# One plan for the attention part and the feed-forward part, and two-operand products of VectorE written as a ScalarE scaling and a sum

## The chip, the cores and the metric

The kernel runs on one core of one Trainium2 chip. The metric is the device time of the kernel in microseconds (us), the median of three runs. TensorE (PE) does the matmuls and the transposes against an identity; VectorE (DVE), ScalarE (ACT) and GpSimd (POOL) do the elementwise work; SyncE (SP) issues nearly all DMAs. An engine runs its instructions in the order in which they stand in its queue, so what a queue holds first is waited for first.

## The reference

One layer of a residual trunk on 2048 rows of width 1024, in float32. Cut to what matters:

```python
u = rms_norm(h, norm1_w)
dq, dk, dv, sq, sk, sv = split(u @ w_in)
# 4 differential heads: two softmax maps per head, T5 position bias, chunk-causal mask
p = softmax(q[c] @ k[c].T * scale + bias)           # c = 0, 1
y_diff = rms_norm((p[0] - lam * p[1]) @ dv)
# 8 stick-breaking heads: strictly causal, no softmax
rem = reverse_cumsum(log_sigmoid(-z)) - log_sigmoid(-z)
y_sb = rms_norm(exp(log_sigmoid(z) + rem) @ sv)
h = h + concat(y_diff, y_sb) @ w_out
u2 = rms_norm(h, norm2_w)
h = h + (silu(u2 @ w_gate) * (u2 @ w_up)) @ w_down   # 1024 -> 2816 -> 1024
```

## The kernel before

**Arithmetic.** A float32 product is made of float16 matmuls: each operand is split into a high half (`hi`, a cast) and a low half (`lo`, operand minus `hi`), and three products are summed in PSUM. Weights are scaled by a power of two first: `split_weight` writes `hi = st * sW` on ACT, DVE or POOL, and `lo = st * sW - hi` with one DVE instruction, SCALAR_TENSOR_TENSOR, which scales its first operand by a per-row value and combines it with a second tensor.

**Attention part.** There are eight groups of heads: groups 0 to 3 are the differential heads (the "diff stage" below), groups 4 to 7 pairs of stick-breaking heads. Rows come in 16 tiles of 128. For each group `load_w` fetches the columns of `w_in` into `wst` and splits them into `w`; `proj_tile` or `proj_turned` projects (`pj` in PSUM), `proj_out` and `proj_batch` normalise and split q and k (`raw` holds four tiles of q and k; `rs` is their reciprocal norm). `diff_attn.probs(i)` handles row tile i: scores `sc` in PSUM, evacuated by DVE into `z` with a running maximum (`mx`), an exponential on ACT with its sum, and then `z0 = z0 + z1 * rc`, which joins the two maps; `split_t` casts the result into `s` (hi), subtracts (lo), and a transposing DMA makes `aT`, which `pv` multiplies with `v` into `yp`. Values of tile i are taken up when two later tiles have been scored. `out_proj` multiplies with `w_out` (`wo`, PSUM `po`, sum in `xf`), and `post` makes from tiles 0 to 11 what the feed-forward part reads (`xcd`).

**Feed-forward part.** Two halves of 8 row tiles, 11 steps of 256 hidden columns each; each 2x2 block product is done with seven products (`quad` for gate and up, `down`). In the first half `load_ffn` fetches each weight into one of two `stages`, squares it on ACT into `sq` (one buffer, used again for sums of the blocks), lets PE sum the columns (`fsc`), finds the scale on DVE, makes the block sums on POOL and splits into `wg`, `wu`, `wd`; it stores the result (`split`), and the second half reads it back. `build_x` does for tiles 12 to 15 what `post` does for the others.

**What sets the order.** In the attention part nothing is issued as it is written. `Recorder` notes every instruction with its reads and writes; `order` then lays them out by a list schedule with prices from `price`, a key (place in the program less a bonus), free buffers, and one more rule: an instruction that `price` marks with `port` (POOL's wide ones, and DVE's wide ones without PSUM operands) starts only when no other such one runs. Where code calls `either` (in `to16`, `tt`, `split_weight`, `split_psum`), the plan picks the engine, by when it would be done there with its price times `KW`. `issue` then emits the instructions in that order. The feed-forward part and tiles 12 to 15 of `out_proj` are outside of the plan: their order comes from the framework's own scheduler, and engines there are chosen by `pick`, which evens out running sums.

Of the kernel before, what the change touches and what calls it, by code (L numbers as in the profile page):

```python
# [40 lines left out]
KW = {"A": 1.0, "D": 2.5, "P": 0.6}  # L41
# [23 lines left out]
class Bank:  # L65


    def __init__(self, rec, pool, shape, dtype, kw):
# [10 lines left out]
        self.readers, self.ops, self.last, self.keep = [], {}, None, False  # L79
# [153 lines left out]
class Recorder:  # L233


    def __init__(self, tc):
        self.tc, self.on, self.ops, self.boost, self.behind, self.open, self.probe = tc, False, [], 0, [], None, None

# [30 lines left out]
    def price(self, eng, name, args, kw):  # L269
# [19 lines left out]
        if eng == "D":  # L289
# [6 lines left out]
            if n <= 16:  # L296
                return 200, None, None, False
# [5 lines left out]
        return (min(190 + 1.91 * n, 430 + 1.45 * n) if name == "tensor_tensor" else 165 + 0.9 * n), None, None, True  # L303
# [90 lines left out]
    def start(self):  # L394
        self.on, self.ops, self.banks = True, [], {}

    def order(self):
        ops = self.ops
        for o in ops:
            o.deps.discard(o.n)  # L400
            o.users, o.left, o.first, o.last, o.after = [], len(o.deps), [], [], 0.0
        for o in ops:
            for d in o.deps:
                ops[d].users.append(o)
        queue, room, held = {}, {}, {}
        for b in sorted(self.banks, key=lambda b: next(iter(b.ops))):
            b.first = ops[next(iter(b.ops))]
            b.first.first.append(b)
            queue.setdefault(b.slot, []).append(b)
            room[b.slot] = b.cap  # L410
            held[b] = len(b.ops)
            for o in b.ops:
                ops[o].last.append(b)
        events = [(0.0, n, "ready", o) for n, o in enumerate(ops) if not o.left]
        heapq.heapify(events)
        count = len(ops)
        ready = {e: [] for e in "TADPS"}
        till = dict.fromkeys(ready, 0.0)
        ring, table, done, shared, want = 0.0, None, [], 0.0, None
# [83 lines left out]
        assert len(done) == len(ops), (len(done), len(ops), [(e, [(o.n, o.calls[0][0].__name__) for o in r[:3]]) for e, r in ready.items()])  # L503
        self.span = now
        return done

    def issue(self):

        done = self.order()
        self.on = False  # L510
        with self.tc.manual_schedule():
            for o in done:
                for f, args, kw in o.calls:
                    o.out = f(*map(true, args), **{k: true(v) for k, v in kw.items()})  # L514


def block(tc, a, out):
# [4 lines left out]
    with top:  # L522
# [59 lines left out]
        make_identity(nc, id32[:])  # L582
        rec.start()
# [82 lines left out]
        def split_weight(hi, lo, st, n, sW, engines="P"):  # L666
# [46 lines left out]
        with ExitStack() as ph1:  # L713
# [38 lines left out]
            def load_w(g, st=None):  # L752
# [12 lines left out]
                for k in range(0, KT, kn):  # L765
                    ks = slice(k, k + kn)
                    split_weight(wv[:, 0, ks, :], wv[:, 1, ks, :], st[:, ks, :], 384 * kn, sW, "ADP" if first else "P")
# [122 lines left out]
            def proj_batch(g, G, B):  # L890
                st, v, raw = B
                qT, kT = new_qk()
                if g < 4:
# [9 lines left out]
                    DVE.tensor_tensor(rq, rq, rsb, ALU.mult)  # L903
# [127 lines left out]
            def diff_attn(g, G):  # L1031
                @pri("at")
                def probs(i):
# [43 lines left out]
                    for (b, n, z0), (_, _, z1) in zip(*zs):  # L1077
                        DVE.scalar_tensor_tensor(z0[:, :n], z1[:, :n], rc[:], z0[:, :n], op0=ALU.mult, op1=ALU.add)
# [255 lines left out]
            def load_wo(n):  # L1334
# [15 lines left out]
                for q, st in enumerate(sts):  # L1350
                    o = slice(D * q, D * q + D)
                    split_weight(hi[:, o], lo[:, o], st[:, :D], D, sW, "AP")
# [8 lines left out]
            def out_proj():  # L1361
                for t in range(NT):
# [20 lines left out]
                    SP.dma_start(hd[t], xf)  # L1383
                    if t >= 12:
                        yield
                        continue
                    post(t, xf)
                    yield

            held = []  # L1390
# [25 lines left out]
            while outs < 12:  # L1416
# [4 lines left out]
        with ExitStack() as ph2:  # L1421
            ps2 = ph2.enter_context(tc.tile_pool(name="ps2", bufs=2, space=PSUM, reuse_waits="tile"))
            fw = ph2.enter_context(tc.tile_pool(name="fw", bufs=2, reuse_waits="tile"))
            xops = {}

            def open_x(os):
                for o in os:
                    xops[o] = ph2.enter_context(tc.tile_pool(name=f"xp{o}", bufs=1, reuse_waits="tile"))
# [464 lines left out]
```

## Time and profile before

| | |
|---|---|
| median of 3 runs | 2657.18 us (2653.93 to 2659.12) |
| the profiled execution's own time | 2652.51 us |
| its span, first to last instruction | 2650.7 us |
| mean granted TensorE clock | 0.988 |
| PE busy | 2475.5 us (93%) |
| DVE busy | 1834.4 us (69%) |
| POOL busy | 1412.5 us (53%) |
| ACT busy | 1224.7 us (46%) |

PE's busy time is nearly the span, so the time that can be had lies in PE's idle 175 us and in stretches at a lower clock. The other engines' shares are means over stages that differ much; they have to be read stage by stage. In the rows of the profile L514 is the line that emits the plan and L220 the line through which all else passes, so instructions are told apart by their tiles.

### The profile page before, as it was taken

Reading aid. Unit: us, or ns where it says so; the run is one execution under the profiler, and the core shown is the slowest. Engines: PE = TensorE matmul, PEld = TensorE weight load, DVE = VectorE, ACT = ScalarE, POOL = GpSimd, SP = SyncE. Lnnn points to the kernel's source line nnn. Section 1 sums busy time; section 2 is a strip of 40 time slices with the busy share of each in tenths; the row PEclk is TensorE's granted clock in tenths of the full one; section 3 lists DMA queues with packets and bytes.
Section 4 is the critical chain, followed back from the end, with each engine's and each line's share of the span. In section 5 each row is a group of like instructions: output and inputs, shape, how many; then the busy total and the mean of one; then the engine's idle time right before and its main releaser. Section 6 shows DMA issues by size and latency. Waiting matters only on the chain.

```text
span 2650.7 us, 50621 instructions
## 1 busy us (share of the span) xinstructions
PE 2475.5 (93%) x19940; PEld 1510.4 (57%) x19940; DVE 1834.4 (69%) x3398; ACT 1224.7 (46%) x2365; POOL 1412.5 (53%) x1093
## 2 busy tenths in 40 slices
PE   6998999989899998899998899999999999999999
PEld 4555556568787875678773344444444444444444
DVE  7888888888888888775557767768685444444434
ACT  4566565656677767664434533435342112111121
POOL 3576675654454545366767757667574232332323
PEclk9999999999999999999998999999999999999999
DMA  7787797876898979888885665565649653545432
GB/s 242 188 181 157 160 191 162 184 155 139 181 189 181 189 175 194 209 189 222 223 321 210 219 225 221 212 230 203 251 170 360 255 210 138 212 152 193 183 112 96
DMA packets 557759, 522.35 MB, mean 197 GB/s; under 512 B 414208, under 2 KB 486400, under 8 KB 547280
## 3 DMA queue, kind: packets, MB, share of 16 engines
q1 hardware_dynamic: 555696, 517.03, 69.3%
q8 instruction: 156, 2.56, 0.4%
q0 software_dynamic: 512, 1.36, 0.1%
q10 hardware_dynamic: 1312, 0.72, 0.1%
q14 instruction: 83, 0.68, 0.1%
HBM read 261.08 MB, written 147.32 MB: 154 GB/s over the span
## 4 chain that ended last, share of the span: by engine, by line
PE 53%; DVE 11%; POOL 8%; DMA 7%; issue 6%; ACT 5%; SPq 0%; DVEq 0%; POOLq 0%; ACTq 0%
PE pd L220 18%; PE pj L514 9%; PE pm L220 8%; PE pa L220 5%; PE sc L514 5%; PE yp L514 4%; DMA aT<-s 3%; DVE z L514 3%; PE po L514 3%; POOL s L514 2%; DVE cg L220 2%; DVE wd L220 2%; ACT z L514 1%; DVE wu L220 1%; POOL sq L220 1%
## 5 line engine op out<-in xcount | busy, mean ns | idle before, releaser
L514 PE MATMUL pj<-w,xt 128*128 128x384 f16 (+1 forms) x3072 | 435.6, 288 | 10.5 <-DVE w L514 6.4
L220 PE MATMUL pd<-wd,act 128*128 128x512 f16 x1764 | 392.5, 380 | 11.1 <-ACT cg L220 4.3
L514 POOL TENSOR_TENSOR s<-z,s 128x512 f16<-128x512 f32 (+7 forms) x231 | 301.2, 1316 | 134.2 <-ACT s L514 113.0
L514 PE MATMUL sc<-kT,qT 128*128 128x512 f16 (+3 forms) x1280 | 320.7, 350 | 31.7 <-DVE z L514 22.4
L514 PEld LDWEIGHTS <-xt 128*128 128x128 f16 x3072 | 255.9, 99 | 142.7 <-issue 18.5
L220 POOL TENSOR_TENSOR act<-cg,act 128x512 f16<-128x512 f32 x126 | 172.8, 1382 | 272.9 <-ACT act L220 160.8
L220 PEld LDWEIGHTS <-wg 128*128 128x128 f16 x1848 | 182.2, 99 | 233.9 <-issue 16.7
L220 PEld LDWEIGHTS <-wu 128*128 128x128 f16 x1848 | 180.6, 98 | 216.2 <-DVE wu L220 2.5
L220 PEld LDWEIGHTS <-act 128*128 128x128 f16 x1764 | 172.8, 98 | 220.8 <-issue 15.2
L514 PE MATMUL yp<-v,aT 128*128 128x64 f16 (+1 forms) x4872 | 235.9, 204 | 28.6 <-DMA aT<-s 17.4
L514 PEld LDWEIGHTS <-aT 128*128 128x128 f16 x4896 | 218.6, 99 | 63.3 <-DMA aT<-s 25.8
L220 POOL TENSOR_TENSOR hs<-hs,cu 128x512 f32<-128x512 f32 x99 | 130.7, 1328 | 171.3 <-DVE hs L220 71.6
L514 POOL TENSOR_TENSOR z<-z,z 128x512 f16<-128x512 f32 (+4 forms) x108 | 117.5, 1090 | 150.3 <-ACT z L514 135.0
L220 ACT CAST act<-cg 128x512 f16<-128x512 f32 x126 | 77.3, 617 | 240.5 <-DVE cg L220 210.2
L220 PE MATMUL pm<-X,wu 128*128 128x512 f16 x792 | 179.9, 379 | 1.5 <-DVE wu L220 1.5
L220 PE MATMUL pm<-X,wg 128*128 128x512 f16 x792 | 180.2, 381 | 0.0
L220 DVE SCALAR_TENSOR_TENSOR hs<-pd,c,hs 128x512 f32<-128x512 f32 x136 | 98.3, 746 | 110.0 <-PE pd L220 81.0
L514 ACT ACTIVATE z<-z,ng 128x1024 f32<-128x1024 f32 (+4 forms) x192 | 170.9, 891 | 3.3 <-ACT ng L514 0.4
L514 DVE TENSOR_TENSOR_SCAN z<-z,sc 128x512 f32<-128x512 f32 x128 | 162.2, 1273 | 14.2 <-ACT z L514 10.7
L514 PEld LDWEIGHTS <-qT 128*128 128x128 f16 x1280 | 113.6, 98 | 99.2 <-issue 32.9
L514 DVE TENSOR_SCALAR_CACHE_REDUCE z<-sc,c 128x512 f32<-128x512 f32 (+3 forms) x256 | 159.9, 649 | 10.6 <-PE sc L514 9.2
L514 PE MATMUL pj<-xt,w 128*128 128x128 f16 x2304 | 152.8, 219 | 13.1 <-DVE qT L514 4.4
(262 smaller groups left out, 4687.3 us busy)
## 6 DMA issues: line engine op xcount, KB each, us to landing
xt<-xs SPq DMA_DIRECT2D x112, 512.0 KB, 4.1
hs<-hd SPq DMA_DIRECT2D x68, 512.0 KB, 4.5
hd<-hs SPq DMA_DIRECT2D x56, 512.0 KB, 4.1
split<-wg SPq DMA_DIRECT2D x11, 1792.0 KB, 8.1
split<-wu SPq DMA_DIRECT2D x11, 1792.0 KB, 6.8
split<-wd SPq DMA_DIRECT2D x11, 1792.0 KB, 7.6
wg<-split SPq DMA_DIRECT2D x11, 1792.0 KB, 7.4
wd<-split SPq DMA_DIRECT2D x11, 1792.0 KB, 11.8
```

The costliest lines, as they stand in the source:

```text
L220: return f(*map(true, args), **{k: true(v) for k, v in kw.items()})
L514: o.out = f(*map(true, args), **{k: true(v) for k, v in kw.items()})
```

## The change

**The plan spans the kernel.** `start` no longer throws away what was recorded. There are three plans one after the other, each starting from the state that the last one left: the attention part with all 16 tiles of `out_proj`; then the first two weights of the feed-forward part (`wg`, `wu` of step 0) and the first six blocks of `X`; then all the rest. Within each plan instructions move freely; on each engine all of one plan stand ahead of the next one's. `w_gate` and `w_up` of step 0 and the six blocks `X` are fetched from ACT's queue, not SP's.

**Products.** For odd row tiles i of the diff stage `z0 + z1 * rc` becomes a scaling of `z1` on ACT and a sum by DVE or POOL, as the plan picks. For groups 1 to 7 of `w_in` and for `w_out`, `split_weight` scales `st` in place on ACT, casts `hi`, and subtracts on DVE or POOL. The product `raw * rs` may go to DVE or POOL.

**Prices.** `KW` of DVE goes from 2.5 to 4 (so a choice shuns DVE more), small DVE instructions from 200 to 220 ns, and POOL's tensor_tensor loses the cheaper slope above some 520 elements.

```diff
-KW = {"A": 1.0, "D": 2.5, "P": 0.6}
+KW = {"A": 1.0, "D": 4, "P": 0.6}
...
-                return 200, None, None, False
+                return 220, None, None, False
...
-        return (min(190 + 1.91 * n, 430 + 1.45 * n) if name == "tensor_tensor" else 165 + 0.9 * n), None, None, True
+        return (190 + 1.91 * n if name == "tensor_tensor" else 165 + 0.9 * n), None, None, True
...
     def start(self):
-        self.on, self.ops, self.banks = True, [], {}
+        self.on, self.base, self.banks, self.open = True, len(self.ops), {}, None
...
-        def split_weight(hi, lo, st, n, sW, engines="P"):
+        def split_weight(hi, lo, st, n, sW, engines="P", spread=False):
+            if spread:
+                ACT.mul(st, st, sW[:])
+                to16(hi, st, n, engines)
+                tt(lo, st, hi, ALU.subtract, n)
+                return
...
-                    DVE.tensor_tensor(rq, rq, rsb, ALU.mult)
+                    tt(rq, rq, rsb, ALU.mult, 1024)
...
-                        DVE.scalar_tensor_tensor(z0[:, :n], z1[:, :n], rc[:], z0[:, :n], op0=ALU.mult, op1=ALU.add)
+                        if i % 2:
+                            ACT.mul(z1[:, :n], z1[:, :n], rc[:])
+                            tt(z0[:, :n], z0[:, :n], z1[:, :n], ALU.add, n)
+                        else:
+                            DVE.scalar_tensor_tensor(z0[:, :n], z1[:, :n], rc[:], z0[:, :n], op0=ALU.mult, op1=ALU.add)
...
-            while outs < 12:
+            while outs < NT:
                 next(op)
                 outs += 1
             rec.issue()
...
         with ExitStack() as ph2:
-            ps2 = ph2.enter_context(tc.tile_pool(name="ps2", bufs=2, space=PSUM, reuse_waits="tile"))
+            rec.start()
+            ps2 = Pool(rec, ph2.enter_context(tc.tile_pool(name="ps2", bufs=2, space=PSUM, reuse_waits="tile")), 2, True)
...
+                q = ACT if f0 == 0 and nme != "d" else SP
...
             load_now(0, 0, "g", W)
-            load_x(0, XL[:3])
-            next(op)
-            next(op)
+            load_x(0, XL[:3], ACT)
             load_now(0, 0, "u", W)
-            load_x(0, XL[3:6])
...
+            load_x(0, XL[3:6], ACT)
+            for dst, xf in late:
+                SP.dma_start(dst, xf)
...
+            rec.issue()
             pjs.close()
+            rec.start()
```

Counted over the built program, PE's instructions are the same in kind and number. Of the 48 products `z0 + z1 * rc` of odd tiles POOL gets 47 sums; POOL gets all 16 of `raw * rs`, all 14 low halves of `w`, and 6 low halves of `wo`; 18 casts into `s` go from POOL to ACT.

**Where it shows, 1: the third diff group, row tile 11.** DVE's queue before, with the two products of this tile (1024 and 512 columns wide) right behind `rc`, and the product `raw * rs` of a projection:

```order
L514 TENSOR_REDUCE sums_5278<-s_5628 128x2
L514 RECIPROCAL rc_5712<-sums_5278 128x1
L514 SCALAR_TENSOR_TENSOR v_5703<-pj_5630,v_5703 128x128
L514 TENSOR_SCALAR rc_5712<-rc_5712,c_347,sums_5278 128x1
L514 SCALAR_TENSOR_TENSOR z_5455<-z_5513,rc_5712,z_5455 128x1024
L514 SCALAR_TENSOR_TENSOR z_5480<-z_5599,rc_5712,z_5480 128x512
L514 TENSOR_TENSOR raw_5390<-raw_5390,rs_5699 128x1024
```

POOL's queue now, where the sums of the same tile stand (`z_5492` and `z_5524` are its two pieces), with a `raw * rs` ahead of the first and splits of q and k between them:

```order
L525 TENSOR_TENSOR rs_5665<-rs_5665,mh_100 128x16
L525 TENSOR_TENSOR raw_5224<-raw_5224,rs_5665 128x1024
L525 TENSOR_TENSOR z_5492<-z_5492,z_5540 128x1024
L525 TENSOR_TENSOR raw_5224<-raw_5224,gk 128x4x128
L525 TENSOR_SCALAR s_5854<-z_5492 128x1024
L525 TENSOR_TENSOR st_5593<-raw_5224,st_5593 128x4x2x64
L525 TENSOR_TENSOR s_5854<-z_5492,s_5854 128x1024
L525 TENSOR_TENSOR st_5593<-raw_5224,st_5593 128x4x2x64
L525 TENSOR_TENSOR z_5524<-z_5524,z_5580 128x512
```

Three wide DVE instructions are gone from behind `rc`; the two sums now stand apart from each other in POOL's queue, and the splits of their results behind them in the same queue.

**Where it shows, 2: the start of the feed-forward part, ACT.** Before, with `sq` the squares of the three weights of step 0 in turn and `x` the last casts of `post`:

```order
L220 ACTIVATE sq_21532<-stages 128x2048
L514 CAST x_21482<-z_21476 128x2x512
L220 ACTIVATE wg_21534<-stages,c_21531 128x2x512
L514 CAST x_21486<-z_21259 128x512
L220 ACTIVATE wg_21534<-sq_21532,c_21531 128x2x512
L220 ACTIVATE sq_21791<-stages 128x2048
```

And now, from the last cast of `post` on (`X` are the blocks that PE reads, `wu` the second weight):

```order
L525 CAST x_21709<-z_21301 128x512
L525 DMA stages<-in_w_gate_dram 128x8x256
...
L525 DMA X_22027<-xcd_73 128x4096
L525 ACTIVATE sq_22031<-stages 128x2048
L525 DMA stages<-in_w_up_dram 128x8x256
L525 ACTIVATE wg_22064<-stages,c_22060 128x2x512
L525 ACTIVATE wg_22064<-sx_22033,c_22060 128x512
L525 ACTIVATE sq_22074<-stages 128x2048
L525 ACTIVATE wu_22102<-stages,c_22099 128x2x512
```

The squares of `wg` and `wu` are still ACT's, but both stand behind all of `post`, and six fetches of `X` stand ahead of the first.

**The same place, PE.** PE's queue now, from the last matmul of `out_proj` (tile 15) to the first product of the feed-forward part (`fsc_22041` are the column sums of `wg`, `fsc_22080` those of `wu`):

```order
L525 MATMUL po_21932<-wo_18551,mt_21690 128x256
L525 LDWEIGHTS ones
L525 MATMUL fsc_22041<-sq_22031,ones 128x256
...
L525 MATMUL fsc_22080<-sq_22074,ones 128x256
L525 LDWEIGHTS wg_22064
L525 MATMUL pa_22129<-X_22017,wg_22064 128x512
```

Before, the column sums of `wg` stood in the middle of tile 13 of `out_proj`, and those of `wu` in that of tile 14, so that matmuls stood between them and the first product; now none does, and both column sums stand ahead of it.

More of the change, by code (lines that the diff above doesn't have):

```diff
@@ L502, in order @@
                 heapq.heappush(events, (end, count, "end", o))
-        assert len(done) == len(ops), (len(done), len(ops), [(e, [(o.n, o.calls[0][0].__name__) for o in r[:3]]) for e, r in ready.items()])
-        self.span = now
+        assert len(done) == len(new), (len(done), len(new), [(e, [(o.n, o.calls[0][0].__name__) for o in r[:3]]) for e, r in ready.items()])
+        self.ring, self.table, self.shared, self.span = ring, table, shared, now
         return done
@@ L510, in issue @@
         self.on = False
[L511 to L514, printed above, removed]
+        for o in done:
+            for f, args, kw in o.calls:
+                o.out = f(*map(true, args), **{k: true(v) for k, v in kw.items()})
 def block(tc, a, out):
@@ L582, in block @@
         make_identity(nc, id32[:])
+        top.enter_context(tc.manual_schedule())
         rec.start()
@@ L1455, in stage @@
                 f0 = 256 * fg
-                with tc.issue_after(rows[1].ins) if (fg, nme) == (1, "u") else nullcontext():
+                with rec.issue_after(rows[1].ins) if (fg, nme) == (1, "u") else nullcontext():
                     fetch(st, f0, nme)
```

81 lines of the change are left out of this document (47 added, 34 removed).

## The prediction

> **What bounds the kernel now.** I read the page's head and its line of busy times first, then busy time by stretches of the span, then PE's waits in each stretch, and last the groups of instructions for prices.
>
> ```profile
> span 2650.7 us, 50621 instructions
> PE 2475.5 (93%) x19940; PEld 1510.4 (57%) x19940; DVE 1834.4 (69%) x3398; ACT 1224.7 (46%) x2365; POOL 1412.5 (53%) x1093
> ...
> 0.00:33.00 33.00, 10.00 (x40) 7.43 (x41) 21.13 (x64) 10.69 (x19) 7.76 (x17) 1.00 0.56 183
> 33.00:640.00 607.00, 549.77 (x4798) 373.07 (x4798) 509.29 (x1474) 371.19 (x909) 375.34 (x282) 0.98 0.79 177
> 640.00:1330.00 690.00, 639.46 (x8951) 524.29 (x8948) 532.57 (x782) 456.37 (x932) 366.90 (x323) 0.99 0.89 193
> 1330.00:1378.00 48.00, 43.81 (x397) 38.72 (x396) 24.98 (x42) 15.07 (x16) 30.41 (x23) 1.00 0.85 306
> 1378.00:1500.00 122.00, 100.64 (x472) 48.16 (x470) 86.41 (x114) 56.53 (x73) 96.96 (x65) 0.90 0.63 238
> 1500.00:2000.00 500.00, 485.74 (x2300) 225.81 (x2299) 370.99 (x542) 200.24 (x238) 337.51 (x232) 1.00 0.60 219
> 2000.00:2651.00 651.00, 646.11 (x2995) 292.91 (x2993) 289.04 (x383) 114.65 (x180) 197.60 (x155) 1.00 0.51 188
> ```
>
> The columns of a stretch are its length, then PE, PEld, DVE, ACT and POOL busy, granted clock, DMA share, GB/s. PE is the bound nearly everywhere, and the change leaves its instructions alone, so all that can move is its idle time: 23 us before its work starts, 57 in the diff stage (33 to 640), 51 in the stick-breaking stage (640 to 1330), 26 in the transition (1330 to 1500, the last `out_proj` tiles and the first feed-forward steps), 14 in the rest of the first feed-forward half, 5 in the second half. In the second half nothing is left to win. In the diff stage DVE is at 84%, POOL at 62%, ACT at 61%. PE's waits there, in the stick-breaking stage, and in the transition:
>
> ```profile
> PE yp L514 <- DMA aT<-s: 13.4, 12, 2.8
> PE sc L514 <- DVE z L514: 6.5, 8, 2.0
> PE sc L514 <- DVE mx L514: 5.3, 6, 1.9
> PE yp L514 <- DVE y L514: 5.3, 4, 3.4
> PE yp L514 <- DVE mo L514: 4.7, 3, 3.5
> PE pj L514 <- DVE w L514: 4.7, 2, 3.6
> PE pj L514 <- DVE c L514: 4.1, 1, 4.1
> ```
> ```profile
> PE sc L514 <- DVE z L514: 18.0, 22, 2.0
> ```
> ```profile
> PE fsc L220 <- ACT sq L220: 9.8, 2, 9.2
> PE pd L220 <- DVE xrs L220: 7.0, 1, 7.0
> PE pd L220 <- DMA X<-xcd: 5.1, 1, 5.1
> PE po L220 <- DVE wo L220: 3.1, 2, 2.2
> ```
>
> The columns are total, times, longest. In the diff stage six rows name DVE, 30.6 us together, and one the transposing DMA behind POOL's subtraction, 13.4. So DVE is what PE waits for most, in many short pieces; a lighter DVE can shorten them.
>
> **Diff stage, DVE's side.** The prices:
>
> ```profile
> L514 DVE SCALAR_TENSOR_TENSOR z<-z,rc,z 128x1024 f32<-128x1024 f32 (+4 forms) x96 | 98.9, 1054 | 1.2
> L514 DVE TENSOR_TENSOR raw<-raw,rs 128x1024 f32<-128x1024 f32 x16 | 19.8, 1236 | 0.8 <-POOL rs L514 0.6
> L514 DVE SCALAR_TENSOR_TENSOR w<-wst,sW,w 128x1536 f16<-128x1536 f32 x8 | 18.1, 2283 | 0.2 <-POOL w L514 0.2
> L514 DVE SCALAR_TENSOR_TENSOR z<-z,xrs,z 128x1024 f32<-128x1024 f32 x13 | 17.4, 1349 | 1.8 <-POOL xrs L514 1.7
> ```
>
> Tile i is 128(i+1) columns wide; the odd i are 72 of the 136 units, so of the 98.9 us 52.4 go. With the 16 `raw` (19.8) and the 8 halves of `w` in this stretch (18.1) DVE loses 90 us: 509 to 419, or 84% to 69%.
>
> **POOL's and ACT's side.**
>
> ```profile
> L514 POOL TENSOR_TENSOR z<-z,z 128x512 f32<-128x512 f32 x12 | 15.3, 1272 | 0.5
> ...
> L514 POOL TENSOR_TENSOR s<-z,s 128x512 f16<-128x512 f32 x114 | 135.5, 1198 | 95.8 <-ACT s L514 89.8 <-issue 5.4
> ...
> L514 POOL TENSOR_TENSOR s<-z,s 128x1024 f16<-128x1024 f32 x40 | 87.5, 2191 | 4.1 <-ACT s L514 3.3
> ...
> L514 POOL TENSOR_SCALAR w<-wst,sW 128x1536 f16<-128x1536 f32 x14 | 23.4, 1676 | 6.5 <-DVE c L514 6.5
> L514 POOL TENSOR_SCALAR s<-z 128x1024 f16<-128x1024 f32 (+7 forms) x58 | 65.4, 1128 | 137.2 <-DVE z L514 128.4 <-DVE ng L514 4.1 <-DMA aT<-s 3.2
> ```
> ```profile
> L514 ACT ACTIVATE z<-z 128x1024 f32<-128x1024 f32 x16 | 16.9, 1060 | 0.9 <-DMA z<-in_x_dram 0.9
> ```
>
> No row has a float32 sum 1024 wide on POOL. 512 wide it took 1.272 us with a float32 result; from 512 to 1024 the float16 form grows by 0.993, which makes 2.27 (bounds: the float16 row, 2.19, and twice 1.272, 2.54; I take 2.27, since the fixed part is paid once). By that slope the 48 sums (36,864 columns) are 71.5 + 48 x 0.279 = 85 us, 83 for the 47 that POOL gets; the 16 `raw` 36; the `w` halves go from 8 x 1.676 to 8 low halves at 3.18 (2.191 + 0.993) and 4 casts at 1.676, +19; 18 casts into `s` leave, -20. POOL gains 118 us: 375 to 493, 81%. ACT gets the 48 scalings (36,864 columns at 1060/1024 ns, 38 us), 12 for `wst`, about 17 in casts: 371 to some 438, 72%. So the load is evened out: 69, 72 and 81% beside PE's 91.
>
> What PE gains: I take half of the 30.6 us that wait for DVE, since the plan packs the engines anew and new near-ties come up; 15. It loses where it waits for `aT`: the chain behind `rc` is now ACT 1.06 + POOL 2.27 where DVE took 1.35 for 1024 columns, 2.0 later, and POOL is fuller. Tile i's values are taken up two tiles later, 2 x 607/64 = 19 us, which covers most; I scale 13.4 by 81/62: +4. Net -11. Bounds: all six DVE rows gone, -31; or each of the 12 waits for `aT` longer by two such chains, +48, with no gain.
>
> **The rule that speaks against it.** POOL and DVE don't run free of each other. DVE's rows, then POOL's:
>
> ```profile
> 1353.89 2.61 DVE L220 SCALAR_TENSOR_TENSOR wg<-sx,c,wg 128x512 f16<-128x512 f32 x1
> ...
> 1372.92 0.74 DVE L220 SCALAR_TENSOR_TENSOR wu<-sx,c,wu 128x512 f16<-128x512 f32 x1
> ```
> ```profile
> 1352.87 5.62 POOL L514 TENSOR_TENSOR x<-z,x 128x1024 f16<-128x1024 f32 x2
> ```
>
> The same form took 0.74 us alone and 2.61 beside two POOL products, which themselves took 5.62 instead of 2 x 2.19. Taken as one resource, POOL's time plus DVE's two-SBUF-operand products in the diff stage were 375 + 98.9 + 19.8 + 18.1 + 17.4 = 529 of 607 us; now 493 + 46.5 + 17.4 = 557. DVE gives up 90 us of this resource and POOL takes 118: the change makes it busier, by 28, past PE's 550. The Trainium skill's page "SBUF — State Buffer", section "Who interferes with whom", states the reason: a DVE instruction with two SBUF inputs and a GpSimd instruction that reads SBUF exclude each other for the whole instruction; by that rule moving a product from one to the other frees nothing, and the stage would not get shorter than 557 us. The two stretched rows agree with it. My 607 - 11 = 596 stays above that floor; the rule gives a rival below.
>
> **Stick-breaking stage.** Six halves of `w` (2.26 each) and eight of `w_out` leave DVE:
>
> ```profile
> 1373.58 1.27 DVE L220 SCALAR_TENSOR_TENSOR wu<-sq,c,wu 128x1024 f16<-128x1024 f32 x1
> ```
>
> At 1.27 for 1024 columns that is 14 + 10 = 24 of DVE's 533 us, 5%. POOL's 367 of 690 has room, so its added sums lie beside other work. Of the 18.0 us for `z` I take 3. Bounds: -18, and +5 if the chain to `w` (in series now on three engines) ends late at a group's first `pj`, as the 4.7 row above shows can be.
>
> **Transition.** Before, the column sums of `wg` and `wu` and DVE's work on them ran beside `out_proj`. Now nothing of PE stands between the last `po` and both `fsc`, and the squares of `wu` wait until DVE has read the sums that live in the same buffer. The chain from the last `po` to the first product:
>
> ```profile
> 1343.59 1.03 PE L220 MATMUL fsc<-sq,ones 128*128 128x256 bf16 x8 [0.60 <-ACT sq L220]
> ...
> 1344.66 0.42 DVE L220 TENSOR_REDUCE m<-fsc 128x1 f32<-128x256 f32 x1 [1.15 <-PE fsc L220]
> ...
> 1345.94 0.20 DVE L220 TENSOR_SCALAR c<-c,c 128x1 f32<-128x1 f32 x1
> ```
> ```profile
> L220 ACT ACTIVATE sq<-stages 128x2048 bf16<-128x2048 f32 x33 | 63.0, 1910 | 78.9 <-issue 25.7 <-DVE wg L220 20.8 <-DVE wd L220 20.1
> ```
> ```profile
> 1372.52 0.47 DVE L220 SCALAR_TENSOR_TENSOR xf<-po,c,xf 128x256 f32<-128x256 f32 x1
> ```
>
> Last eviction 0.47, `fsc` 1.03, reduction to scale 1.48 (1344.66 to 1346.14), cast on ACT 1.06, three low halves 3 x 1.27, squares 1.91, `fsc` 1.03: 10.8 us, of which PE works 2.1. That is 8.7 idle (13 if each low half is stretched as above). Against it the waits for `wo` (3.1) go, as no split stands ahead of the evictions; `X`'s (5.1) goes too, since PE comes to its seventh product later than the fetch can be asked for. The 7.0 and the 9.2 came while POOL was busy 97 of 122 us; the work displaced behind `out_proj` does not lighten that, but PE's orders are planned now: I keep 11 of 16. Sum 8.7 - 3.1 - 5.1 - 5 = -5. Bounds: all but 8.7 gone, -16; or nothing gone and 13 added, +13.
>
> **Rest of the feed-forward part.** Its order is the plan's now, with prices under the rows (`price` gives 1168 ns for the 512 sum that took 1272). 14 us idle; I take no change, bounds -8 and +20 (11 steps, 2 us each late). Second half: DVE 44%, covered.
>
> **Sum.** -11 - 3 - 5 = -19 on the profiled execution's 2652.5: 2633.5. The median of the runs shown, 2657.2, is 4.7 above that execution; as a median I say 2636. What this measurement can tell from no change is some 0.2%, 5 us.
>
> **Rivals.** (a) *Shared resource, slower.* POOL's sums and DVE's remaining products block each other, and the odd tiles' `aT` come late. Place: `yp` in the diff stage, tiles 8 to 15. It decides once the stage's 557 us, stretched by some 10% as in the rows above, passes 607: 557 x 1.1 = 613, +6, and each of the 12 waits 1 to 2 us longer, +18; with -8 from elsewhere 2657 + 16 = 2673. For it: the sum above PE's 550. Against: 33 to 640 lived with 529. 0.12. (b) *The plan is worse than the framework's scheduler* in the feed-forward part: +20 there, -14 elsewhere: 2663. Against: at 1500 to 2000 DVE is 74% busy, POOL 68%. 0.08. (c) *Gain eaten*: each DVE wait is replaced by another; within 5 us of 2657. 0.12. (d) *Larger gain*: all DVE rows gone (-31), -12 in the second stage, -16 in the transition: 2598. 0.13. (The built order shows POOL taking the sums, so that the change does not happen is no rival.) My forecast, 2615 to 2652: 0.55.
>
> Faster 0.68, same 0.12, slower 0.20. The range 2603 to 2671 leaves out (d)'s and (a)'s outer halves and little else; the forecast alone, 2615 to 2652.
>
> **What would show it.** Right: DVE near 70% and POOL near 80% in the diff stage; its idle PE down by some 10 us, with more of it on `aT`; a gap of 8 to 13 us ahead of the first `pa`, and no wait for `X`; the second half as before. Wrong: a diff stage as long as before with products on both engines stretched (a), waits for `fsc` and `pd` in every step (b).

## The result, and the profile after

The changed kernel took 2616.65 us (median of 4 runs, 2613.42 to 2617.57), the kernel before 2655.55 (4 runs): ratio 0.9854, 95% interval 0.9832 to 0.9876. The profiled execution, the fastest of the four, took 2613.42 us. Its page and the stretches of its span, with the columns and bounds of the table of before:

```profile
span 2611.6 us, 50674 instructions
PE 2464.5 (94%) x19940; PEld 1503.8 (58%) x19940; DVE 1721.6 (66%) x3308; ACT 1308.0 (50%) x2466; POOL 1533.4 (59%) x1152
...
33.00:640.00 607.00, 565.35 (x5166) 390.03 (x5167) 459.07 (x1441) 464.06 (x1043) 481.91 (x330) 0.99 0.81 183
640.00:1330.00 690.00, 648.74 (x8898) 532.42 (x8896) 498.56 (x747) 456.52 (x912) 406.22 (x339) 1.00 0.89 204
1330.00:1378.00 48.00, 36.25 (x197) 20.05 (x196) 24.83 (x47) 14.80 (x18) 20.93 (x17) 0.86 0.66 249
1378.00:1500.00 122.00, 104.21 (x494) 48.79 (x493) 92.93 (x124) 55.70 (x70) 105.84 (x70) 0.94 0.56 202
```

Fixed stretches no longer hold the same work (the first scores of the stick-breaking stage come at 586.2 us, before at 618.2). So I also compare kernels at equal work: each matmul is given the usual distance to its successor, and a kernel's progress is the sum over the matmuls it has started, of 2416 us in all. Four segments by that measure: up to 600 (the diff stage and what leads to it), 600 to 1180 (stick-breaking), 1180 to 1300 (transition), the rest. For the first, PE's idle time and the loss at half clock (half of the time at granted clock 0.5, an upper bound, since PE idles in part of it) stand beside it. All in us, one profiled execution each:

| kernel | median | to 600 | idle, half clock | 600 to 1180 | to 1300 | rest |
|---|---|---|---|---|---|---|
| before | 2655.55 | 716.3 | 88.3, 13.7 | 644.7 | 151.0 | 1134.0 |
| after | 2616.65 | 683.5 | 65.3, 5.1 | 639.2 | 159.1 | 1124.6 |
| e1 products back | 2630.94 | 685.3 | 65.7, 10.2 | 651.1 | 159.6 | 1126.9 |
| e2 odd sums on DVE | 2644.39 | 701.2 | 75.8, 17.1 | 650.0 | 162.4 | 1126.7 |
| e3 raw and w back | 2635.44 | 694.7 | 71.8, 18.8 | 647.0 | 158.7 | 1126.9 |
| e4 prices back | 2635.30 | 678.4 | 60.5, 11.9 | 658.0 | 164.8 | 1124.8 |
| e5 span alone | 2663.79 | 716.9 | 84.2, 25.6 | 654.5 | 164.2 | 1129.7 |
| e6 no span | 2619.11 | 678.1 | 62.1, 1.7 | 641.8 | 150.3 | 1136.1 |
| e7 raw and w alone | 2625.14 | 682.8 | 66.9, 5.1 | 650.0 | 148.7 | 1137.4 |
| e8 products, all tiles | 2643.84 | 712.3 | 83.8, 23.9 | 645.5 | 159.8 | 1126.9 |
| e9 raw alone | 2647.09 | 709.6 | 81.9, 13.7 | 642.3 | 151.0 | 1135.6 |
| e10 w alone | 2636.22 | 698.8 | 72.9, 11.9 | 649.4 | 151.6 | 1135.5 |
| e11 yrs seen by plan | 2678.87 | 724.6 | 91.1, 25.6 | 661.7 | 159.2 | 1126.9 |
| e12 wu later | 2612.56 | 678.2 | 60.5, 8.5 | 641.3 | 157.3 | 1126.9 |

e12 and the changed kernel have the same order up to the last matmul of `out_proj`, and still differ by 5.3 us in the first segment. So I read nothing into less than some 5 us of one segment. A profiled execution can also lie off its kernel's median: those of e5 and e8 were the slowest of their kernels, 8.5 and 7.7 us above it, that of e10 stood 5.8 above, that of e6, the fastest, 6.2 below.

The change gained 33 us in the diff stage (23 idle, 9 half clock), 5.5 in the second, 9 in the rest of the feed-forward part, and lost 8 in the transition. The 5.5 are at the limit of what can be read. PE's waits in the diff stage of the changed kernel, 33 to 607 us (total, times, longest):

```profile
PE yp L525 <- DMA aT<-s: 16.1, 12, 3.2
PE sc L525 <- DVE mx L525: 3.8, 6, 1.0
PE sc L525 <- DVE z L525: 3.4, 5, 1.3
PE sc L525 <- DMA qT<-qT: 3.2, 3, 1.7
PE pj L525 <- POOL w L525: 2.1, 3, 1.5
```

The rows that named `w`, `c`, `y` and `mo` of DVE (18.8 us before) are gone, what the scores wait for `z` and `mx` is down from 11.8 to 7.2, and the transposed tiles cost 2.7 more than the 13.4 of before.

The transition, PE from the last matmuls of `out_proj` to the first product, then ACT and DVE in the gap (start, duration, idle before and its releaser in brackets):

```profile
1339.46 1.05 PE L525 MATMUL fsc<-sq,ones 128*128 128x256 bf16 x8 [0.72 <-DVE ones L525]
1350.38 1.87 PE L525 MATMUL fsc<-sq,ones 128*128 128x256 bf16 x8 [9.87 <-ACT sq L525]
1352.04 4.77 PE L525 MATMUL pa<-X,wg 128*128 128x512 f16 x12
```
```profile
1341.94 1.15 ACT L525 ACTIVATE wg<-stages,c 128x1024 f16<-128x1024 f32 x1 [12.88 <-DVE c L525]
...
1348.42 1.91 ACT L525 ACTIVATE sq<-stages 128x2048 bf16<-128x2048 f32 x1 [4.72 <-DVE wg L525]
```
```profile
1343.12 3.93 DVE L525 SCALAR_TENSOR_TENSOR wg<-stages,c,wg 128x1024 f16<-128x1024 f32 x2 [0.97 <-ACT wg L525]
1346.98 1.27 DVE L525 SCALAR_TENSOR_TENSOR wg<-sq,c,wg 128x1024 f16<-128x1024 f32 x1
```

This is the chain of the prediction link by link: scale, cast, three low halves, and only then the squares of `wu`, whose buffer the third low half had read. The two column sums stand back to back in PE's order, so the gap is 9.9 us. From 1342.5 us, inside the gap, to 1356.1, behind it, the clock stood at 0.50:

```profile
1342.50:1356.10 13.60, 5.72 (x18) 2.60 (x18) 8.21 (x11) 4.88 (x5) 10.22 (x9) 0.50 0.47 169
```

PE's waits in the last `out_proj` tiles (the first row, 1300 to 1500 us) and from 1378 to 1500 us:

```profile
PE po L525 <- DVE wo L525: 2.9, 5, 0.6
```
```profile
PE pd L525 <- POOL wd L525: 6.4, 1, 6.4
PE pd L525 <- DVE cg L525: 4.0, 1, 4.0
PE pd L525 <- DVE wd L525: 2.2, 2, 1.6
```

### The profile page after: what moved, and what is told of

It reads as the page before. It is cut to its first block, busy times and chain, and to the rows that moved or that the text cites. A ratio compares the mean times of both kernels' runs of the same rounds, so it can differ in the third digit from the quotient of the medians.

```text
span 2611.6 us, 50674 instructions
## 1 busy us (share of the span) xinstructions
PE 2464.5 (94%) x19940; PEld 1503.8 (58%) x19940; DVE 1721.6 (66%) x3308; ACT 1308.0 (50%) x2466; POOL 1533.4 (59%) x1152
## 4 chain that ended last, share of the span: by engine, by line
PE 70%; DVE 8%; POOL 8%; DMA 6%; issue 4%; ACT 3%; SPq 0%; DVEq 0%; POOLq 0%; ACTq 0%
PE pd L525 22%; PE pm L525 11%; PE pj L525 11%; PE pa L525 8%; PE po L525 6%; PE sc L525 5%; PE yp L525 4%; POOL s L525 3%; DMA aT<-s 3%; DVE z L525 2%; DMA aT<-z 1%; POOL z L525 1%; DVE cg L525 1%; ACT z L525 1%; DVE wd L525 1%
## 5 line engine op out<-in xcount | busy, mean ns | idle before, releaser
L525 PE MATMUL sc<-kT,qT 128*128 128x512 f16 (+3 forms) x1280 | 319.4, 349 | 25.6 <-DVE z L525 14.8
L525 POOL TENSOR_TENSOR z<-z,z 128x512 f16<-128x512 f32 (+8 forms) x155 | 206.7, 1337 | 169.8 <-ACT z L525 152.8
L525 PE MATMUL yp<-v,aT 128*128 128x64 f16 (+1 forms) x4872 | 236.3, 203 | 22.6 <-DMA aT<-s 16.3
L525 POOL TENSOR_TENSOR hs<-hs,cu 128x512 f32<-128x512 f32 x99 | 138.9, 1416 | 157.7 <-DVE hs L525 88.9
L525 DVE TENSOR_SCALAR_CACHE_REDUCE z<-sc,c 128x512 f32<-128x512 f32 (+3 forms) x256 | 161.1, 650 | 35.7 <-PE sc L525 17.7
L525 PEld LDWEIGHTS <-mt 128*128 128x128 f16 x1536 | 148.8, 98 | 37.2 <-issue 15.8
```

## The experiments

Theories after the result: A, the diff stage gains because DVE carries less; B, because of the new prices; C, the shared resource of POOL and DVE decides. Later: L, what counts is `raw` and `w`, on which the next group's projections hang; S, the long plan orders the stage better.

**e1, the odd products back on DVE.**

```diff
-                        if i % 2:
-                            ACT.mul(z1[:, :n], z1[:, :n], rc[:])
-                            tt(z0[:, :n], z0[:, :n], z1[:, :n], ALU.add, n)
-                        else:
-                            DVE.scalar_tensor_tensor(z0[:, :n], z1[:, :n], rc[:], z0[:, :n], op0=ALU.mult, op1=ALU.add)
+                        DVE.scalar_tensor_tensor(z0[:, :n], z1[:, :n], rc[:], z0[:, :n], op0=ALU.mult, op1=ALU.add)
```

> The changed kernel with one part undone: for odd row tiles z0 + z1 * rc is one DVE instruction again; the span of the plan, the raw and w moves and the prices stay. Between the two kernels the first scores of the stick-breaking stage come 32 us earlier (618.2 to 586.2 us from the span's start), where I had forecast 11. Theory A (DVE's load decides): the odd products are 52 of the 90 us that left DVE in the diff stage, so it gives back 52/90 x 32 = 18 us: scores at 604 and 2635 us in all, DVE near 505 of 607 us again. Theory B (the new prices make a better plan, the products are beside the point): within 5 us of 2617. Theory C (POOL and DVE's two-SBUF products share one resource, and the change won in spite of POOL's added 83 us): faster than 2617, by up to 83 - 52 = 31 us, the amount by which that resource gets lighter.

Measured 2630.94 us, ratio 0.9914 (0.9902 to 0.9926). The total is near A's, but the place is wrong: the diff stage lost 1.8 us, not 18. The 12 us are in the second stage, where this edit changes no instruction, and only the packing of the plan differs. So with `raw` and `w` moved, the products bring the diff stage nothing that can be read.

**e2, the odd sums forced to DVE.**

```diff
-                            tt(z0[:, :n], z0[:, :n], z1[:, :n], ALU.add, n)
+                            tt(z0[:, :n], z0[:, :n], z1[:, :n], ALU.add, n, "D")
```

> The changed kernel with the scaling of z1 left on ACT, but the sums of odd tiles forced to DVE as tensor_tensor instead of left to the plan (which gave POOL 47 of 48). DVE then carries about as many wide two-SBUF instructions as before, POOL 83 us less. Theory A (DVE's load decides): as with the products back, 16 to 20 us slower than 2617: 2635, scores at 604. Theory B (prices): within 5 us of 2617. Theory C (shared resource): not slower, POOL's 83 us leave the resource and some 48 come back, so 2617 or below. A fourth, D: what won is the split in two (scale early on an idle engine, a shorter last step), then about 2617 to 2622 with DVE at 80%.

Measured 2644.39 us, 0.9961 (0.9946 to 0.9976): slower than every theory's number, so C and D fall. The diff stage lost 17.7 us against the changed kernel, and the wait that grew is that for the transposed tiles (33 to 610 us; the changed kernel has 16.1):

```profile
PE yp L525 <- DMA aT<-s: 23.5, 17, 3.7
```

Against e1 the work on DVE is the same to the eye, a sum in place of a product, with one hand-over from ACT more in the chain to `aT`; the stage is 16 us longer. So the 17.7, though A's number for this stage, do not come from DVE's load. Here splitting the product paid only where its second half left DVE too.

**e3, `raw * rs` and `split_weight` back.**

```diff
-                    split_weight(wv[:, 0, ks, :], wv[:, 1, ks, :], st[:, ks, :], 384 * kn, sW, "ADP", not first)
+                    split_weight(wv[:, 0, ks, :], wv[:, 1, ks, :], st[:, ks, :], 384 * kn, sW, "ADP" if first else "P")
...
-                    tt(rq, rq, rsb, ALU.mult, 1024)
+                    DVE.tensor_tensor(rq, rq, rsb, ALU.mult)
...
-                    split_weight(hi[:, o], lo[:, o], st[:, :D], D, sW, "AP", True)
+                    split_weight(hi[:, o], lo[:, o], st[:, :D], D, sW, "AP")
```

> The changed kernel with raw * rs back on DVE and split_weight as before (no scaling in place on ACT, low half by one DVE instruction); odd products, span and prices stay. Theory A (DVE's load decides): 38 of the 90 us of the diff stage and 24 us of the stick-breaking stage go back to DVE: 38/90 x 32 = 13 us lost in the first, some 4 of the 8 us that the second had gained: 2634 in all, scores at 599. Theory B (prices): within 5 us of 2617. Theory C (shared resource): POOL loses some 36 + 19 us and DVE gets 38, a lighter resource: 2617 or below.

Measured 2635.44 us, 0.9933 (0.9921 to 0.9945), A's number. The diff stage lost 11.2 us and kept 21.6 of the 33: the products (with the new prices) do work when `raw` and `w` stay on DVE. In PE's waits from 33 to 610 us a row is back that the changed kernel doesn't have:

```profile
PE pj L525 <- DVE w L525: 5.9, 1, 5.9
```

**e4, the three old prices.**

```diff
-KW = {"A": 1.0, "D": 4, "P": 0.6}
+KW = {"A": 1.0, "D": 2.5, "P": 0.6}
...
-                return 220, None, None, False
+                return 200, None, None, False
...
-        return (190 + 1.91 * n if name == "tensor_tensor" else 165 + 0.9 * n), None, None, True
+        return (min(190 + 1.91 * n, 430 + 1.45 * n) if name == "tensor_tensor" else 165 + 0.9 * n), None, None, True
```

> The changed kernel with the three old prices: KW of DVE 2.5, small DVE instructions 200 ns, POOL's tensor_tensor cheaper above 520 elements. Theory A (DVE's load decides): a weight of 2.5 sends some of the choices back to DVE; up to a third of the moved 90 us, so 2617 to 2628, and DVE busier by the same share. Theory B (prices make the plan): most of the 32 us is lost, 2640 to 2650, with DVE's busy time in the diff stage little changed. If it is within 5 us of 2617 at the same DVE load, the prices are not what won.

Measured 2635.30 us, 0.9936 (0.9923 to 0.9949). The diff stage was as short as with the new prices (678.4), so B falls there. The 19 us are lost from 600 on: 18.8 in the second stage, 5.7 in the transition. e1 to e4 all lose 8 to 19 us in the second stage, though e1 and e2 change no instruction there; the changed kernel's plan is the shortest there of all that ran. What makes it so I can't say.

**e5, the span alone.** The changed kernel with the edits of e1, e3 and e4 together.

> The changed kernel with the odd products, raw * rs, split_weight and the prices all put back: the one plan over the whole kernel is left. Measured against equal amounts of PE's work done, the changed kernel reaches the end of the diff stage 33 us earlier than before: 23 us less idle, 9 us less at half clock. Theory A (the lighter DVE): all of that goes, the stage takes as long as before, first scores of the stick-breaking stage near 618 us; the span alone gives -4 to -8 us in the feed-forward part less some 5 to 14 lost at its first product, so 2645 to 2660 in all. Theory S (a longer plan also orders the diff stage better): scores near 586 to 600, 2617 to 2635.

Measured 2663.79 us, 1.0034 (1.0023 to 1.0046): slower than before, and slower than A's upper end. The diff stage is that of before (716.9, in the slowest of twelve executions), so S falls. The transition lost 13 us, the second stage 10, the rest gained 4.

**e6, everything but the span.** The kernel before with the products, the new `split_weight`, `raw * rs` and the prices of the diff in the section on the change; `start`, the 12 tiles and the second part as before.

> The kernel before with all the products and prices of the change, but the old three-part order (12 tiles of out_proj in the plan, the rest and the feed-forward part by the framework's scheduler). Theory A (products and raw and w make the diff stage): scores of the stick-breaking stage at 586 to 590 as in the changed kernel; the start of the feed-forward part is as before, without the 9.9 us wait for the squares of wu, so it gains some 10 there and loses some 10 later (fsc, pd and the rest of the first half): 2612 to 2628. Theory S (the span matters to the diff stage): scores near 600 to 618 and 2630 to 2650.

Measured 2619.11 us (2612.92 to 2625.67), 0.9861 (0.9843 to 0.9879), not to be told from the changed kernel. It has the short diff stage. Against it the span costs 8.8 us in the transition and gains 11.5 in the rest. Most of the 11.5 are in PE's waits from 1490 to 2010 us, here and then in the changed kernel, and in two more stretches at half clock:

```profile
PE pd L220 <- ACT cg L220: 4.3, 2, 3.6
PE pd L220 <- DVE hs L220: 4.2, 2, 2.7
PE pd L220 <- DVE cg L220: 2.3, 4, 1.5
PE pm L220 <- DVE wu L220: 1.5, 2, 0.8
PE fsc L220 <- ACT sq L220: 1.1, 2, 0.6
```
```profile
PE pd L525 <- DVE cg L525: 5.0, 4, 2.5
PE pd L525 <- DVE hs L525: 1.0, 1, 1.0
PE pd L525 <- ACT cu L525: 0.7, 2, 0.5
```

**e7, `raw` and `w` alone.** The kernel before with the new `split_weight`, its two calls, and `tt(rq, rq, rsb, ALU.mult, 1024)`; nothing else.

> The kernel before with raw * rs left to the plan and split_weight in its new form; no odd products, old prices, no span. DVE loses some 38 us of 607 in the diff stage, 84% to 78 to 82%. The run with the products back lost only 2 us of the 33 by the end of the diff stage, at DVE 82%. Theory L (latency: what counts is that raw * rs and w, on which the next group's projections hang, no longer queue on DVE): 25 to 33 us of the diff stage are here already, scores near 587 to 593, 2620 to 2632 in all. Theory A (load of DVE in proportion): 38/90 of 33, 14 us, scores near 604, 2640.

Measured 2625.14 us, 0.9881 (0.9865 to 0.9897): L. The diff stage is as short as in the changed kernel. From 100 to 500 us, before, after, and here:

```profile
100.00:500.00 400.00, 365.32 (x2883) 233.69 (x2882) 338.72 (x1029) 249.49 (x630) 270.56 (x197) 0.98 0.80 171
```
```profile
100.00:500.00 400.00, 374.59 (x3006) 241.23 (x3005) 303.98 (x1044) 313.25 (x723) 349.03 (x233) 0.99 0.83 178
```
```profile
100.00:500.00 400.00, 374.69 (x3025) 243.00 (x3024) 345.94 (x1081) 273.46 (x670) 305.11 (x215) 0.99 0.83 179
```

DVE is busier here than before (346 of 400 us against 339), and PE gets as much done as in the changed kernel, where DVE has 304. A share of time alone does not settle it, since more work was done in these 400 us. So I compare DVE's busy time over the first segment, from 33 us to its end: before, here, and in e3, where the products have moved and `raw` and `w` have not:

```profile
33.00:716.00 683.00, 617.69 (x5842) 431.92 (x5842) 569.87 (x1559) 421.65 (x1017) 405.44 (x310) 0.98 0.79 176
```
```profile
33.00:683.00 650.00, 605.12 (x5882) 425.84 (x5881) 546.29 (x1544) 444.06 (x1031) 448.22 (x323) 0.99 0.82 186
```
```profile
33.00:695.00 662.00, 613.16 (x5884) 431.40 (x5885) 527.70 (x1513) 469.40 (x1087) 467.39 (x341) 0.98 0.81 182
```

e7 takes 24 us off DVE and gains 33.5; e3 takes 42 and gains 21.6. How much leaves DVE is not what decides; A falls. That `raw` and `w` bring the whole gain is shown. Why is in part argued: of PE's waits from 33 to 690 us the rows that named `w` and `c` of DVE (9.2 us) are gone, as L has it, but the scores' wait for `z` fell by 4.8 too and that for `mo` by 3.0. No run moved `w` ahead in DVE's queue and left it there, which would tell its place in the queue from its length.

**e8, the products split in all tiles** (`if True:` in place of `if i % 2:`).

> The changed kernel with z0 + z1 * rc split into a scaling on ACT and a sum in even row tiles too; the plan gives POOL 46 of the 48 further sums. POOL's time in the diff stage rises by some 72 us (64 units of 136, as the 72 units of odd tiles cost 83) from 482 to some 555 of 607, 91%, DVE falls by 46 to some 410, and POOL with DVE's two-SBUF products, taken as one resource, from 100 to 109 us per 100 us of the stage to above that. Shared resource: the stage gets 10 to 30 us longer, scores at 596 to 616, yp waits for aT longer. Theory A (DVE decides): no slower than 2617. Theory R (DVE has enough relief already and POOL is not full): scores within 6 us of 586.

Measured 2643.84 us, 0.9959 (0.9944 to 0.9974): slower than the changed kernel, at the long end of what was expected. The diff stage took 28.8 us longer (by the medians the whole kernel took 27.2 longer). Its 100 to 500 us, and PE's waits on DVE from 33 to 610 us:

```profile
100.00:500.00 400.00, 367.41 (x2891) 236.82 (x2889) 265.96 (x970) 332.75 (x726) 374.51 (x254) 0.97 0.81 172
```
```profile
PE sc L525 <- DVE mx L525: 13.2, 7, 7.4
PE sc L525 <- DVE z L525: 9.6, 6, 3.1
```

POOL is at 94%, DVE down to 66%, and PE waits for DVE again, since DVE waits for POOL. DVE's waits on POOL from 33 to 610 us, here and then in the changed kernel:

```profile
DVE z L525 <- POOL z L525: 32.1, 25, 4.2
DVE z L525 <- POOL s L525: 28.0, 20, 2.8
```
```profile
DVE z L525 <- POOL s L525: 13.2, 16, 2.4
...
DVE z L525 <- POOL z L525: 7.9, 11, 1.8
```

These are the evacuations of scores into `z`. DVE stands idle ahead of them, with no instruction of its own begun, until POOL has done the sums and splits that read a buffer of `z`: 60 us against 21. POOL's instructions take no longer than in the changed kernel (a sum 1024 wide 2362 ns in both), there are more of them. That points to POOL's backlog and not to the shared resource. Nor did the sum of POOL's busy time and DVE's two-SBUF rows rise, as was expected: per 100 us from 200 to 500 us it is 98 to 103 here and 101 to 108 in the changed kernel. The resource has one place of its own: the 7.4 us were behind a `yrs` of 4 elements, two operands in SBUF, that took 7.88 us.

**e9 and e10, `raw` alone, `w` alone.** The kernel before with one of e7's two edits each.

> The kernel before with raw * rs alone left to the plan (POOL takes it): 16 instructions, 20 us, leave DVE; split_weight, products, prices and order rules as before. Raw and w together, without anything else, made the diff stage 33 us shorter. Theory A (in proportion to the DVE time that leaves): 20/38 of it, 17 us, 2640. Theory L (what counts is w, on which the next group's projections hang, and whose low half is the longest DVE instruction, 2.28 us): 5 to 12 us, 2645. Theory F (near a threshold: the first relief of DVE, whichever, takes most of the waits): 22 to 30 us, 2628 to 2635.

> The kernel before with split_weight alone in its new form (groups 1 to 7 of w_in and w_out): some 18 us leave DVE in the diff stage. Theory A (proportion): 18/38 of 33, 16 us, 2640. Theory L (w is what counts): 22 to 30 us, 2628 to 2635. Theory F (any first relief takes most): 22 to 30 us as well, so that the two alone add up to far more than the 33 of both together.

Measured 2647.09 us, 0.9972 (0.9961 to 0.9983), and 2636.22, 0.9933 (0.9919 to 0.9948). In the diff stage `raw` brought 6.7 us, `w` 17.5, both 33.5. F falls (the two do not replace each other), A's equal shares do not fit; the order is L's, `w` the larger, though L had it at 22 to 30. With `raw` alone PE still waits for the weights (33 to 690 us):

```profile
PE pj L514 <- DVE w L514: 11.6, 4, 3.8
```

That both bring 9 us more than the sum of each I cannot explain from these runs; one profile differs from another by 5.

**e11, the small `yrs` marked for the plan**, on top of e8.

```diff
-                return 220, None, None, False
+                return 220, None, None, name == "scalar_tensor_tensor"
```

> The kernel with the products split in all tiles (2644 us), and one price changed: DVE's SCALAR_TENSOR_TENSOR of 16 elements or fewer (the 16 yrs<-yss,er, two operands in SBUF) is marked as a user of the shared resource, so the plan starts it only when no wide POOL instruction runs. In the kernel with all tiles split one yrs of 4 elements took 7.88 us, from POOL's first to its last of a run of back-to-back instructions, and PE waited 7.4 us behind it for mx. Theory Y (this unseen collision is a large part of that kernel's loss): 10 to 18 us of the 27 come back, 2626 to 2634. Theory P (POOL is simply too full, 86 to 91%): within 6 us of 2644, with PE waiting as long for mx and z of DVE, which wait for POOL.

Measured 2678.87 us, 1.0088 (1.007 to 1.0106): slower than before, and neither Y nor P. The mark didn't prevent the collision; I take it that the plan's times were not the chip's, and nothing ties POOL's queue to DVE's. DVE, then POOL's run at that time, then PE:

```profile
162.91 10.21 DVE L525 SCALAR_TENSOR_TENSOR yrs<-yss,er 128x4 f32<-128x4 f32 x1
```
```profile
162.65 1.30 POOL L525 TENSOR_TENSOR raw<-raw,gk 128x512 f32<-128x512 f32 x1
...
170.96 2.15 POOL L525 TENSOR_TENSOR s<-z,s 128x1024 f16<-128x1024 f32 x1
```
```profile
173.78 1.12 PE L525 MATMUL yp<-id,y 128*128 128x128 f32 x4 [8.22 <-DVE y L525]
```

Why the rest of this plan is worse than e8's, 12 us in the first segment and 16 in the second, stays open.

**e12, the second weight later.**

```diff
-            load_now(0, 0, "u", W)
+            wu0 = load_ffn(0, 0, "u", W)
+            next(wu0)
             load_x(0, XL[3:6], ACT)
...
             rec.start()
+            for _ in wu0:
+                pass
             open_x(XL[6:])
```

> The changed kernel with the second weight of the first step (its squares, column sums, scale and split) moved from the second plan to the head of the third, so that products with wg may stand ahead of its column sums on PE; its fetch stays. Up to the last matmul of out_proj the order is the same. Theory T (the wait of 9.9 us ahead of the first product is due to both column sums standing ahead of it): the chain is now column sums, scale 1.48, cast 1.06, a low half 1.27, so 4 to 5 us idle are left, and the half clock that follows is one stretch of 3.4 us shorter: 6 to 9 us less, 2608 to 2611. Rival: the products with wu now wait for it instead, within 3 us of 2617.

Measured 2612.56 us (2610.44 to 2616.61), 0.9845 (0.9831 to 0.9859). It beats the kernel before; from the changed kernel it can't be told. T was right on the gap, which fell from 9.9 to 2.6 us, and wrong on the total: the next weights are late instead, with a half clock from 1386.4 to 1396.6 us behind.

```profile
1340.00 1.03 PE L525 MATMUL pa<-X,wg 128*128 128x512 f16 x2 [2.64 <-ACT wg L525]
```
```profile
1390.86 1.03 PE L525 MATMUL pa<-X,wg 128*128 128x512 f16 x2 [3.72 <-POOL wg L525]
```

The first product came 12 us earlier than in the changed kernel, the second step's 2.3. But `out_proj` had ended 3.1 us earlier here, in an order that is the same up to there; so of the 12 the edit brought 9, and at the second step nothing was left of them.

## Why the prediction was right, and where it was not

The forecast's side, its main place and its range held: 2616.65 lies just inside 2615 to 2652. On the profiled execution the sum was -19 and the outcome -39.1. That the total stayed inside is partly luck: the diff stage brought 22 us more than forecast and the rest of the feed-forward part 9 more, and the transition took 13 of them back. (The sum's 2633.5 and the offset of 4.7 make 2638, not 2636 as the prediction has it; nothing hangs on that.)

- **Diff stage, -11 against -33: the term that was mis-sized.** "I take half of the 30.6 us that wait for DVE" was too little, and there was no term for the clock. Idle time fell by 23 us, and half clock took 9 us less. The bound of -31, all DVE rows gone, was nearer. The reason given, a lighter DVE (84% to 69%), is not what decided: e7 has the whole gain with 24 us off DVE, e3 two thirds of it with 42 off. What counted most were the weights and `raw`, which the prediction took only as DVE load; its row `pj <- DVE w` pointed there. The products, with the new prices, bring 21.6 us where these stay on DVE (e3) and nothing that can be read beyond them (e1). The six rows were not all of DVE's either: `v`, `qT` and `xt` below them held 7.0 us more. The +4 for longer waits on `aT` was 2.7.
- **POOL's and ACT's side held roughly.** POOL was forecast at 493 us in 33 to 640 and had 482, ACT at 438 and had 464; over the first segment POOL gained 97 us, where 118 were forecast. The prices:

```profile
L525 POOL TENSOR_TENSOR z<-z,z 128x1024 f32<-128x1024 f32 x24 | 56.6, 2362 | 34.1 <-ACT z L525 25.2 <-DVE c L525 8.8
L525 POOL TENSOR_TENSOR w<-wst,w 128x1536 f16<-128x1536 f32 x14 | 43.5, 3110 | 0.0
L525 POOL TENSOR_TENSOR raw<-raw,rs 128x1024 f32<-128x1024 f32 x16 | 30.5, 1904 | 0.4
```

  2.36 for a forecast 2.27, 3.11 for 3.18, 30.5 for 36. DVE at 459 was over the forecast 419, partly since the stretch now holds some 33 us of the next stage; over the first segment it lost 75 us, where 90 were forecast.
- **Stick-breaking stage, -3 against -5.5**: inside the bounds and too small to read.
- **Transition, -5 against +8.1.** The gap was forecast at 8.7 to 13 and is 9.9, and the wait for `X` went, as forecast. The waits for `wo` did not: 2.9 us in five pieces, where 3.1 were to go. And "I keep 11 of 16" failed: in place of the 7.0 for `xrs` and the 9.2 for `sq` stand 8.6 for `wd`, 4.0 for `cg` and smaller ones of up to 0.9 us, so hardly anything was won there. PE's idle time in this segment went from 22.6 to 29.5 us, its time at half clock from 23.9 to 27.3, of which 13.7 lie in and behind the large gap.
- **Rest of the feed-forward part, 0 against -9.4**, past the bound of -8: idle fell from 13.5 to 6.9. e6 shows that this is the span's work, as the loss in the transition is; against e6 the two nearly cancel.
- **Rival (a), the shared resource, did not come.** The changed kernel had 101 to 108 us of POOL's and DVE's two-SBUF work in each 100 us from 200 to 500 us (summed over their rows; over 100 means that waiting is inside the rows), the kernel before 90 to 101 and e7 100 to 105, so the sum does not tell the faster from the slower. e8 shows what comes at twice the dose: not this rival, but POOL's own queue. The rule of the Trainium skill ("SBUF — State Buffer", "Who interferes with whom") agrees with the `yrs` rows of the last section; the floor of 557 us that the prediction worked out from it was not put to the test, as the stage still took some 574 (33 to 607).
- **Rival (b) did not come** (fewer waits in the feed-forward part), **(c) neither**; **(d)** was right on the diff stage and wrong on the other two.

## What to carry to other kernels

An engine's busy share says little about who waits for it: ask which of its instructions the bound engine's next work hangs on, and move those first (here `w`, and `raw` with it). Undo the parts of a change singly and together, and find the place of each loss, since the planned order here lost 11 to 12 us in a stage where the edit changes no instruction (e1, e2), and a total then credits the wrong part. When work moves to a neighbour, look for the dose at which its own queue fills: here between half of the products and all of them.

## What the runs showed of the hardware

**A wait of PE costs more than its length.** The granted clock changes on a fixed grid of 3.41 us. I summed PE's idle time in each such window of full clock in all fourteen traces. 134 windows held more than 2.06 us, and each was followed by half clock for one window or more; with less than 1.48 us none was; in between it went either way (41 were, 117 were not). It is the sum in the window that counts, not one gap, and a gap that straddles two windows may go free: one of 3.61 us in e10, from 1722.9 us, fell on two windows with 1.92 and 1.69 and neither was followed by half clock. Ahead of the last 10 us the kernel before ran 61.4 us at half clock, which lost at most half of that, 31 us; after, it was 44.4 us, at most 22. The Trainium skill's page "TensorE: Matmul & The Clock Gate" (Part 1 on the clock gate) gives the same free-running window, but asks for an idle window of some 3.4 us; here some 2 us of idle in it were enough.

**A small DVE instruction with two SBUF operands waits for POOL's instruction, and now and then for a run of them.** A `yrs` has four elements per row and takes 0.14 us at its shortest. In the fourteen traces 105 of them met a POOL instruction with the next one back to back behind it, and 102 of these ended within 0.06 us of the first one's end. So here, in e1 (DVE, then POOL):

```profile
628.99 2.61 DVE L525 SCALAR_TENSOR_TENSOR yrs<-yss,er 128x4 f32<-128x4 f32 x1
```
```profile
628.47 3.10 POOL L525 TENSOR_TENSOR w<-wst,w 128x1536 f16<-128x1536 f32 x1
631.53 1.15 POOL L525 TENSOR_TENSOR z<-z,z 128x512 f16<-128x512 f32 x1
```

The other three were passed over at such an end: the 10.21 us of e11, from POOL's instruction at 162.65 to the end of the last of its run at 173.11, past seven ends, and two of e8, 7.88 us past three ends and 5.08 past two. What tells these from the others stays open; they came in the two kernels in which POOL is fullest. What the small size saves is the work, not the wait.
